# Queries over the ALiBi slope, and one VectorE operation that adds the distance, multiplies by the slope and gathers the rows' greatest attention scores

## The chip, the core and the metric

The kernel runs on one core of a Trainium2 chip. Its engines work side by side and wait for each other by semaphores: TensorE (PE in the profile; its weight loads are PEld), VectorE (DVE), ScalarE (ACT), GpSimd (POOL) and SyncE (SP, which issues most DMAs). The metric is device time in microseconds for one execution of the whole program.

## What is computed

One step of a hybrid decoder layer for a prompt of 512 rows and 64 sample rows (8 sequences of 8): a modulated RMSNorm, one input projection, a gated short convolution beside a sliding-window attention, a merge by gates, an output projection, then a convolutional feed-forward block. The change concerns the attention alone: 16 query heads in 4 groups of 4, a window of 128 keys, a penalty that grows with the distance (ALiBi, one slope per head) and one learned sink per head:

```
s = jnp.einsum('...qhgd,...khd->...hgqk', q, k).astype(jnp.float32) * (HEAD_DIM ** -0.5)
s = s - _alibi_slopes()[:, :, None, None] * dist[..., None, None, :, :]
s = jnp.where(valid[..., None, None, :, :], s, NEG_INF)
m = jnp.maximum(jnp.max(s, axis=-1, keepdims=True), sink)
p = jnp.exp(s - m)
p = p / (jnp.sum(p, axis=-1, keepdims=True) + jnp.exp(sink - m))
```

## The kernel before

Activations lie transposed (features on the 128 partitions, 576 columns of tokens). Each product with a weight matrix runs as three products of high and low parts, so every weight tile is first split: ScalarE rounds the high part (`whi`), VectorE or a DMA that adds makes the low part (`wlo`). TensorE runs nearly without a pause, in the order in which the program is written (`pinned` keeps it so); the order on VectorE, ScalarE and GpSimd is set by a scheduler that simulates the program while it is built.

The attention runs as a filler between the matmuls of the input projection. `tick` is called after each group of six matmuls and lets the generator `attention` take a step at a fixed rate. The prompt part has 16 turns: 4 key heads times 4 blocks of 128 queries (block 0 has 128 keys, the others 256). In each turn `prompt_scores` multiplies 4 query heads by the keys into two PSUM tiles (`aux`) and makes 4 score tiles `s` by one VectorE operation per head, which multiplies the distance table `nd` (minus the distance, or a very large negative number where a key is not allowed) by the slope and adds the scores. `softmax_exps` reduces them to the rows' greatest values, negated (`nmx`), takes the minimum with the negated sinks, runs four exponentials on ScalarE that also sum up the rows (`den`), and one for the sink (`es`); `divide` multiplies the scores by 1/`den`. A turn later `prompt_turn` transposes `s` on TensorE, and a turn after that `prompt_values` multiplies by the values. After the prompt, two decode passes for the sample rows do the same with tables of their own (`nds`, slopes `slo` and sinks `snks` per partition).

`queries` makes the attention's queries from the projection: it scales the product into a high part on ScalarE, the low part on VectorE, and an unsplit copy for the sample rows on VectorE (`qS`, `qX`). A DMA on GpSimd's queue puts the low part beside the high one.

Lines that the text speaks of: the score operations are lines 1096 (prompt) and 1025 (decode), the reductions 954, the minimum 957, the exponentials 960, the sink's exponential 966 with its input `es` on line 965, the sum 969, the reciprocal 970, the division 972. The transposes and all operations that go through a recording helper have line 115; value products have line 1122. ScalarE's first tap of the convolution is `y<-pad`, VectorE's taps are operations that read and write `y`.

Of the kernel before, what the change touches and what calls it, by code (L numbers as in the profile page):

```python
# [10 lines left out]
F32 = mybir.dt.float32  # L11
F32R = mybir.dt.float32r
AF = mybir.ActivationFunctionType
# [62 lines left out]
def step_kernel(ctx: ExitStack, tc: tile.TileContext, ins: dict, outs: list):  # L76
# [19 lines left out]
    def slot(s, dt=F32, shape=None):  # L96
        return ap_.tile(shape or [P, NT], dt, tag="a", name=nm(s))
# [4 lines left out]
    def aux():  # L102
        return pa.tile([P, 512], F32, tag="aux", name=nm("aux"))
# [27 lines left out]
    def pv(t):  # L131
        return t[:, 0:512]
# [671 lines left out]
    def key_parts(hd):  # L804
# [5 lines left out]
            nc.gpsimd.dma_start(x[other].bitcast(F32), x[mine].bitcast(F32))  # L810
        KS[hd] = kh, kl

    def queries(t, ps=None):

        scale = HD**-0.5 if ps is None else 1.0
        if ps is None:
            ps = product(weights(kpm(w_in, Q0 + t * P), NK), h)
        low = slot("low", F32R, [P, 512])
        hd, g2 = t // 2, t % 2
        qq = [slot("q", F32R, [P, 512]) for _ in range(2)]  # L820
        for par in range(2):
            nc.scalar.activation(qq[par][HALF[par]], pv(ps)[HALF[par]], AF.Copy, scale=scale)
        for par in range(2):
            q, mine, other = qq[par], HALF[par], HALF[1 - par]
            nc.vector.scalar_tensor_tensor(
                out=low[mine], in0=pv(ps)[mine], scalar=scale, in1=q[mine].bitcast(F32),
                op0=ALU.mult, op1=ALU.subtract,
            )
            nc.gpsimd.dma_start(q[other].bitcast(F32), low[mine].bitcast(F32))
            QS[4 * hd + 2 * g2 + par] = q  # L830
            ready[hd] = ticks[0] + Q_TICKS
            dst = qS[:, hd // 2, :, :, par, g2, :] if par == hd % 2 else qX[:, hd // 2, :, :, g2, :]
            nc.vector.tensor_scalar(
                out=dst[mine], in0=sv(ps)[mine].rearrange("p (q b t) -> p q b t", q=2, b=4),
                scalar1=scale, scalar2=None, op0=ALU.mult,
            )
# [69 lines left out]
    nds = con2[:, 0:512].rearrange("p (q c) -> p q c", q=2)  # L906
    ind = con2[:, 512:516]
    slo = con2[:, 516:520]
    nsnk = cp.tile([P, 16], F32, tag="nsnk", name="nsnk")
    nc.vector.tensor_scalar(out=nsnk, in0=snk, scalar1=-1.0, scalar2=None, op0=ALU.mult)  # L910
    snks = cp.tile([P, 4], F32, tag="snks", name="snks")
    sel = cp.tile([P, 4, 4], F32, tag="sel", name="sel")
    nc.vector.tensor_tensor(
# [3 lines left out]
        op=ALU.mult,  # L917
    )
    nc.vector.reduce_sum(out=snks, in_=sel, axis=AX.X)
    nsnks = cp.tile([P, 4], F32, tag="nsnks", name="nsnks")  # L920
    nc.vector.tensor_scalar(out=nsnks, in0=snks, scalar1=-1.0, scalar2=None, op0=ALU.mult)
    par2 = cp.tile([74, P], F32, tag="par2", name="par2")
    for dst, src in (
        (par2[:66], ins["ffn_conv_w"].rearrange("o a (r c) -> (o a r) c", c=P)),
# [18 lines left out]
    pinned.append(pe)  # L943
    ot = [wp.tile([P, 4, NT], F32, tag="oh", name=nm("o"), bufs=2) for _ in range(2)]

    def softmax(s, n, sinks, nsinks, w):
        softmax_exps(s, n, sinks, nsinks, w)()

    def softmax_exps(s, n, sinks, nsinks, w):


        nmx = sp.tile([P, n], F32, tag="nmx", name=nm("nmx"))
        for x in range(n // 2):
            nc.vector.tensor_reduce(
                out=nmx[:, 2 * x : 2 * x + 2], in_=s[x][:, :, :w], axis=AX.X, op=ALU.max, negate=True
            )
        nc.vector.tensor_tensor(out=nmx, in0=nmx, in1=nsinks, op=ALU.min)
        den = sp.tile([P, n], F32, tag="den", name=nm("den"))
        for x in range(n):
            nc.scalar.activation(  # L960
                s[x // 2][:, x % 2, :w], s[x // 2][:, x % 2, :w], AF.Exp,
                bias=nmx[:, x : x + 1], accum_out=den[:, x : x + 1],
            )
# [12 lines left out]

        return divide
# [13 lines left out]
    def decode_scores(q, s, cV):  # L991
        kTc = []
        for raw, v in (caches[q][:2], caches[q][2:]):
            cV.append(v)
            a = aux()
            for b in range(2):
                for j in range(2):
                    at = (b * 2 + j) * P
                    transpose(a[:, at : at + P], raw[:, b, j * P : j * P + P], ident)
            t = slot("kTc", shape=[P, 2, 2, P])  # L1000
            nc.scalar.copy(t.rearrange("p b j w -> p (b j w)"), a)
            kTc.append(t)
            yield False
        s += [slot("s", shape=[P, 2, 256]) for _ in range(2)]
        S = [aux() for _ in range(2)]
        for j in range(2):
            at = j * 256
            lhs = qS[:, j, q].rearrange("p b x g t -> p (b x g t)")
            for b in range(4):
                for hf in range(2):  # L1010
                    matmul(
                        S[hf][32 * b : 32 * b + 32, at : at + P],
                        lhs[HALF[hf], 32 * b : 32 * b + 32],
                        kTc[b // 2][HALF[hf], b % 2, j, :],
                        start=True, stop=True,
                    )
            for hf in range(2):
                matmul(
                    S[hf][:, at + P : at + 2 * P], lhs[HALF[hf]], tok_cols(kT[j][HALF[hf]], 4),
                    start=True, stop=True,  # L1020
                )
        for j in range(2):
            for hf in range(2):
                hd, at = 2 * j + hf, j * 256
                nc.vector.scalar_tensor_tensor(
                    out=s[j][:, hf, :], in0=nds[:, q, :], scalar=slo[:, hd : hd + 1],
                    in1=S[hf][:, at : at + 256], op0=ALU.mult, op1=ALU.add,
                )
        yield False
        divide = softmax_exps(s, 4, snks, nsnks, 256)  # L1030
        yield False
        yield False
        divide()
        yield False
# [48 lines left out]
    def prompt_scores(hd, i, ss):  # L1083
        w = 256 if i else P
        k0 = (i - 1) * P if i else 0
        ss += [slot("s", shape=[P, 2, 256]) for _ in range(2)]
        kh, kl = (x[:, k0 : k0 + 256] for x in KS[hd])
        for x in range(2):
            S = aux()
            for e in range(2):  # L1090
                q = QS[4 * hd + 2 * x + e][:, i * P : i * P + P]
                dst = S[:, e * 256 : e * 256 + 256]
                matmul(dst, q, kh, start=True, stop=False)
                matmul(dst, q, kl, start=False, stop=True)
            for e in range(2):
                nc.vector.scalar_tensor_tensor(
                    out=ss[x][:, e, :w], in0=nd[:, 256 - w : 256],
                    scalar=2.0 ** (-8.0 * (4 * hd + 2 * x + e + 1) / 16),
                    in1=S[:, e * 256 : e * 256 + w], op0=ALU.mult, op1=ALU.add,
                )  # L1100

    def prompt_turn(hd, i, ss):
# [32 lines left out]
    def attention():  # L1135
# [3 lines left out]
        for n in range(19):  # L1139
            arg = (n // 4, n % 4) if n < 16 else None  # L1140
            if n in CACHE_AT:
                cache_load(CACHE_AT.index(n))
            if arg:
                yield from prompt_ready(*arg)
            ready_values = turned
            turned = (*waiting[:2], prompt_turn(*waiting)) if waiting else None
            waiting, scored = scored, (*arg, []) if arg else None
            if arg:
                prompt_scores(*scored)
            yield False  # L1150
            if ready_values:
                prompt_values(*ready_values)
            if arg:
                h4 = slice(4 * arg[0], 4 * arg[0] + 4)
                softmax(scored[2], 4, snk[:, h4], nsnk[:, h4], 256 if arg[1] else P)
            yield False
        filler[1] = CX_RATE
        waiting = None
# [1025 lines left out]
```

## Time and profile before

| | |
|---|---|
| median of 3 runs | 975.87 us (975.84 to 975.96) |
| the profiled execution | 975.77 us |
| its span, first to last instruction | 974.0 us |
| TensorE matmul busy | 960.2 us (99%) |
| VectorE busy | 699.9 us (72%) |
| ScalarE busy | 529.8 us (54%) |
| GpSimd busy | 156.9 us (16%) |
| TensorE's granted clock, mean of the span | 0.997 |

The page also follows the chain of work that ended last back from the last instruction; 95% of it is TensorE. A busy share is an average over the span, so the timelines are needed to see who waits where. Starts in a timeline are us from the span's start; neighbouring instructions of one engine overlap a little, so that four in a row take less than four times one.

### The profile page before, as it was taken

What the parts mean: (1) busy time and instruction counts of PE and PEld (TensorE: products, weight loads), DVE (VectorE), ACT (ScalarE), POOL (GpSimd) and SP (SyncE); (2) the same over time, 40 slices, a digit from 0 to 9 for tenths busy, and PEclk for the clock granted to TensorE, in tenths of its full rate; (3) what the DMA queues carried; (4) which work ended last, traced back from release to release, by engine and by line L of the source; (5) the groups of instructions that cost most, each with busy time, mean ns of one, the idle gap of its engine ahead of it and who ended that gap; (6) DMA issues with size and microseconds to landing.
All of it is one profiled execution on the core that took longest, in us unless ns stands there. A gap on an engine that the chain in (4) does not pass through costs nothing.

```text
span 974.0 us, 18976 instructions
## 1 busy us (share of the span) xinstructions
PE 960.2 (99%) x7396; PEld 924.6 (95%) x7396; DVE 699.9 (72%) x1359; ACT 529.8 (54%) x968; POOL 156.9 (16%) x349
## 2 busy tenths in 40 slices
PE   7999999999999999999999999999999999999997
PEld 5899999999999889999899999999999999999996
DVE  5555877777968658897588687784568873578753
ACT  6365667656654435665343568662347652256553
POOL 2132222111212000011000131220013220022120
PEclk9999999999999999999999999999999999999998
DMA  9994345464466772478953454672447762556502
GB/s 302 318 265 123 97 96 124 107 192 106 124 151 182 228 236 86 112 154 223 355 195 90 123 126 98 159 179 87 117 124 169 165 162 66 133 135 166 131 9 98
DMA packets 183563, 148.82 MB, mean 153 GB/s; under 512 B 8007, under 2 KB 161966, under 8 KB 183186
## 3 DMA queue, kind: packets, MB, share of 16 engines
q1 hardware_dynamic: 169954, 108.83, 36.6%
q0 software_dynamic: 13088, 38.00, 19.3%
q8 instruction: 58, 0.95, 0.4%
q10 hardware_dynamic: 432, 0.79, 0.2%
q14 instruction: 31, 0.25, 0.1%
HBM read 109.17 MB, written 7.35 MB: 120 GB/s over the span
## 4 chain that ended last, share of the span: by engine, by line
PE 95%; DMA 2%; issue 1%; SPq 1%; DVE 0%; POOL 0%; ACT 0%; POOLq 0%; DVEq 0%
PE mm L115 64%; PE aux L115 28%; PE aux L1223 2%; PE aux L1122 1%; DMA ad<-in_w_ada 1%; SPq L437 1%; DMA x<-in_x_prompt 1%; POOL r L115 0%; ACT hh L115 0%; DVE hl L115 0%; DVE yo L115 0%; POOLq L2180 0%; DVEq L2180 0%; DVE xn L115 0%; DVE modT L115 0%
## 5 line engine op out<-in xcount | busy, mean ns | idle before, releaser
L115 ACT ACTIVATE whi<-raw 128x1024 fp32r<-128x1024 f32 (+2 forms) x176 | 179.8, 1031 | 94.5 <-PE mm L115 46.7
L115 DVE TENSOR_TENSOR wlo<-raw,whi 128x1024 fp32r<-128x1024 f32 (+2 forms) x133 | 157.0, 1183 | 52.3 <-ACT whi L115 50.7
L115 POOL DMA_DIRECT2D wlo<-raw x43 | 37.7, 876 | 374.4 <-ACT wlo L115 203.7
L115 PE MATMUL mm<-hh,whi 128*128 128x256 f32 (+2 forms) x392 | 92.4, 302 | 0.6 <-ACT hh L115 0.6
L115 PE MATMUL mm<-hh,wlo 128*128 128x256 f32 (+2 forms) x392 | 89.4, 294 | 0.0
L115 PE MATMUL mm<-hl,whi 128*128 128x256 f32 (+2 forms) x392 | 88.1, 295 | 0.3 <-DVE hl L115 0.2
L115 PE MATMUL mm<-th,whi 128*128 128x288 f32 x296 | 87.8, 297 | 0.0
L115 PE MATMUL mm<-tl,whi 128*128 128x288 f32 x296 | 87.2, 295 | 0.0
L115 PE MATMUL mm<-th,wlo 128*128 128x288 f32 x296 | 87.2, 295 | 0.0
L115 PEld LDWEIGHTS mm<-hh,whi 128*128 128x128 f32 x392 | 65.8, 188 | 9.1 <-issue 7.5
L115 PEld LDWEIGHTS mm<-hh,wlo 128*128 128x128 f32 x392 | 67.2, 188 | 0.3 <-DVE wlo L115 0.3
L115 PEld LDWEIGHTS mm<-hl,whi 128*128 128x128 f32 x392 | 66.1, 188 | 1.0 <-DVE hl L115 1.0
L115 PE MATMUL mm<-fh,whi 128*128 128x256 f32 (+1 forms) x304 | 65.4, 296 | 0.0
L115 PE MATMUL mm<-fl,whi 128*128 128x256 f32 (+1 forms) x304 | 65.3, 296 | 0.0
L115 PE MATMUL mm<-fh,wlo 128*128 128x256 f32 (+1 forms) x304 | 64.8, 294 | 0.0
L115 DVE SCALAR_TENSOR_TENSOR x<-mm,modT,x 128x512 f32<-128x512 f32 (+1 forms) x29 | 19.6, 677 | 62.2 <-PE mm L115 62.0
L115 PEld LDWEIGHTS mm<-th,whi 128*128 128x128 f32 x296 | 55.6, 188 | 0.8 <-issue 0.8
L115 PEld LDWEIGHTS mm<-tl,whi 128*128 128x128 f32 x296 | 55.7, 188 | 0.0
L115 PEld LDWEIGHTS mm<-th,wlo 128*128 128x128 f32 x296 | 55.7, 188 | 0.0
L115 DVE TENSOR_TENSOR raw<-raw 128x512 f32<-128x512 f32 x74 | 51.2, 692 | 2.5
L115 PEld LDWEIGHTS mm<-fh,wlo 128*128 128x128 f32 x304 | 51.0, 188 | 0.0
L115 PEld LDWEIGHTS mm<-fl,whi 128*128 128x128 f32 x304 | 50.9, 189 | 0.0
(369 smaller groups left out, 2915.7 us busy)
## 6 DMA issues: line engine op xcount, KB each, us to landing
raw<-in_w_in SPq DMA_DIRECT2D x52, 512.0 KB, 4.7
raw<-in_w_up SPq DMA_DIRECT2D x44, 512.0 KB, 4.3
wlo<-raw POOLq DMA_DIRECT2D x43, 512.0 KB, 4.7
ada<-in_w_ada SPq DMA_DIRECT2D x64, 256.0 KB, 5.6
ad<-in_w_ada SPq DMA_DIRECT2D x32, 256.0 KB, 5.9
raw<-in_w_down SPq DMA_DIRECT2D x16, 512.0 KB, 4.1
wl<-s POOLq DMA_DIRECT2D x27, 256.0 KB, 4.3
raw<-in_w_conv_out SPq DMA_DIRECT2D x8, 512.0 KB, 4.5
```

Of the source, the lines that this page charges most:

```text
L115: done = getattr(self.engine, name)(*args, **kwargs)
L437: return tc.keep_in_program_order(queue.dma_start(dst, src))
L1122: done = nc.tensor.matmul(O[HALF[par], :256], vt(i - nkt + 1 + kt)[:, hd * 64 : hd * 64 + 64], pts[kt][:, par * 256 : par * 256 + 256], st ...
L1223: done = nc.tensor.matmul(ps[32 * j : 32 * j + 32, :], cT[:, k, :], cols[k][j], start=(k == 1), stop=(k == NK - 2),)
```

## The change

The queries are divided by the head's slope where they are scaled, so that TensorE gives scores over the slope. A new helper `biased` replaces the scale-and-add operation: it adds the distance table, multiplies by the slope, and gathers in the same pass the greatest value of each row, starting from the sink, into a column of `mx`. `softmax_exps` takes `mx` times -1 instead of the reductions and the minimum. The negated copies of the sinks (`nsnk`, `nsnks`) go.

```diff
+    def slope(head):
+        return 2.0 ** (-8.0 * (head + 1) / 16)
...
-            nc.scalar.activation(qq[par][HALF[par]], pv(ps)[HALF[par]], AF.Copy, scale=scale)
+            nc.scalar.activation(
+                qq[par][HALF[par]], pv(ps)[HALF[par]], AF.Copy, scale=scale / slope(2 * t + par)
+            )
...
-                out=low[mine], in0=pv(ps)[mine], scalar=scale, in1=q[mine].bitcast(F32),
+                out=low[mine], in0=pv(ps)[mine], scalar=scale / slope(2 * t + par),
+                in1=q[mine].bitcast(F32),
...
-                scalar1=scale, scalar2=None, op0=ALU.mult,
+                scalar1=scale / slope(2 * t + par), scalar2=None, op0=ALU.mult,
...
-    nc.vector.tensor_scalar(out=nsnk, in0=snk, scalar1=-1.0, scalar2=None, op0=ALU.mult)
...
-    nc.vector.tensor_scalar(out=nsnks, in0=snks, scalar1=-1.0, scalar2=None, op0=ALU.mult)
...
+    def biased(out, dist, scores, slopes, sink, greatest):
+        nc.vector.tensor_tensor_reduce(
+            out=out, in0=dist, in1=scores, scale=slopes, scalar=sink, op0=ALU.add, op1=ALU.max,
+            accum_out=greatest,
+        )
...
-        for x in range(n // 2):
-            nc.vector.tensor_reduce(
-                out=nmx[:, 2 * x : 2 * x + 2], in_=s[x][:, :, :w], axis=AX.X, op=ALU.max, negate=True
-            )
-        nc.vector.tensor_tensor(out=nmx, in0=nmx, in1=nsinks, op=ALU.min)
+        nc.vector.tensor_scalar(out=nmx, in0=mx, scalar1=-1.0, scalar2=None, op0=ALU.mult)
...
-                nc.vector.scalar_tensor_tensor(
-                    out=s[j][:, hf, :], in0=nds[:, q, :], scalar=slo[:, hd : hd + 1],
-                    in1=S[hf][:, at : at + 256], op0=ALU.mult, op1=ALU.add,
+                biased(
+                    s[j][:, hf, :], nds[:, q, :], S[hf][:, at : at + 256], slo[:, hd : hd + 1],
+                    snks[:, hd : hd + 1], mx[:, hd : hd + 1],
                 )
...
-                nc.vector.scalar_tensor_tensor(
-                    out=ss[x][:, e, :w], in0=nd[:, 256 - w : 256],
-                    scalar=2.0 ** (-8.0 * (4 * hd + 2 * x + e + 1) / 16),
-                    in1=S[:, e * 256 : e * 256 + w], op0=ALU.mult, op1=ALU.add,
+                y = 2 * x + e
+                biased(
+                    ss[x][:, e, :w], nd[:, 256 - w : 256], S[:, e * 256 : e * 256 + w],
+                    slope(4 * hd + y), snk[:, 4 * hd + y : 4 * hd + y + 1], ss[2][:, y : y + 1],
                 )
```

TensorE's instructions and SyncE's are the same, in the same order, in both programs. On the other engines the scheduler orders some anew. Three places, all in block 2 of head 0, are shown; the numbers behind names are buffers, and differ between the programs.

VectorE, from the last score operation of block 2 to the next convolution tap, before:

```order
L1096 SCALAR_TENSOR_TENSOR s_1267<-con_927,aux_1275 128x256 x2
L954 TENSOR_REDUCE nmx_1300<-s_1266 128x2
L954 TENSOR_REDUCE nmx_1300<-s_1267 128x2
L1340 TENSOR_TENSOR pad_1318<-mm_1210,c_1018 128x512
L1341 TENSOR_TENSOR pad_1318<-mm_1210,c_1018 128x8x8
L115 TENSOR_TENSOR wlo_1704<-raw_1701,whi_1703 128x1024
L957 TENSOR_TENSOR nmx_1300<-nmx_1300,nsnk 128x4
L115 SCALAR_TENSOR_TENSOR y_1325<-pad_1318,parT,y_1325 128x592
```

and after (`ISA` is the new operation; it is followed each time by a second instruction that writes one column of `mx`):

```order
L952 ISA s_1261,mx_1262<-con_927,aux_1270,snk 128x256
L952 ISA mx_1262 128x1
L964 TENSOR_SCALAR nmx_1295<-mx_1262 128x4
L1350 TENSOR_TENSOR pad_1311<-mm_1206,c_1014 128x512
L1351 TENSOR_TENSOR pad_1311<-mm_1206,c_1014 128x8x8
L972 TENSOR_TENSOR es_1302<-snk,nmx_1295 128x4
L115 TENSOR_TENSOR wlo_1694<-raw_1691,whi_1693 128x1024
L115 SCALAR_TENSOR_TENSOR y_1318<-pad_1311,parT,y_1318 128x592
```

The greatest value `nmx` stood behind a weight split and now stands ahead of it, straight behind the last of four such pairs.

ScalarE at the same place, from a weight's high part to the copies of the transposed block before, before:

```order
L115 ACTIVATE whi_1703<-raw_1701 128x1024
L115 ACTIVATE y_1325<-pad_1318,parT 128x592
L115 ACTIVATE kh_1329<-kT_727 64x512
L960 ACTIVATE s_1266,den_1304<-s_1266,nmx_1300 128x256 x2
L960 ACTIVATE s_1267,den_1304<-s_1267,nmx_1300 128x256 x2
L1113 COPY pt_1371<-aux_1366 128x512
L966 ACTIVATE es_1309<-es_1309 128x4
```

and after:

```order
L115 ACTIVATE whi_1693<-raw_1691 128x1024
L967 ACTIVATE s_1260,den_1297<-s_1260,nmx_1295 128x256 x2
L967 ACTIVATE s_1261,den_1297<-s_1261,nmx_1295 128x256 x2
L115 ACTIVATE y_1318<-pad_1311,parT 128x592
L115 ACTIVATE kh_1322<-kT_727 64x512
L973 ACTIVATE es_1302<-es_1302 128x4
L1122 COPY pt_1364<-aux_1359 128x512
```

The four exponentials moved ahead of the convolution's first tap (`y`) and the key split (`kh`).

VectorE from block 3's last scores to block 2's division, before:

```order
L1096 SCALAR_TENSOR_TENSOR s_1381<-con_927,aux_1389 128x256 x2
L969 TENSOR_TENSOR den_1304<-den_1304,es_1309 128x4
L954 TENSOR_REDUCE nmx_1418<-s_1380 128x2
L954 TENSOR_REDUCE nmx_1418<-s_1381 128x2
L970 RECIPROCAL den_1304<-den_1304 128x4
L957 TENSOR_TENSOR nmx_1418<-nmx_1418,nsnk 128x4
L972 TENSOR_SCALAR s_1266<-s_1266,den_1304 128x256 x2
L972 TENSOR_SCALAR s_1267<-s_1267,den_1304 128x256 x2
```

and after, the start of this stretch and its end:

```order
L115 TENSOR_TENSOR kl_1323<-kT_727,kh_1322 64x512
L976 TENSOR_TENSOR den_1297<-den_1297,es_1302 128x4
L952 ISA s_1373,mx_1375<-con_927,aux_1376,snk 128x256
L952 ISA mx_1375 128x1
```

```order
L952 ISA s_1374,mx_1375<-con_927,aux_1383,snk 128x256
L952 ISA mx_1375 128x1
L977 RECIPROCAL den_1297<-den_1297 128x4
L964 TENSOR_SCALAR nmx_1412<-mx_1375 128x4
L979 TENSOR_SCALAR s_1260<-s_1260,den_1297 128x256 x2
L979 TENSOR_SCALAR s_1261<-s_1261,den_1297 128x256 x2
```

The sum `den`, which waits for ScalarE, moved ahead of block 3's score operations, and the second convolution tap stands between their pairs; the reductions are gone.

## Rows read from the trace of the kernel before

**Rows 1.** The page, part 1: busy us (share of the span) x instructions, each engine.

```profile
PE 960.2 (99%) x7396; PEld 924.6 (95%) x7396; DVE 699.9 (72%) x1359; ACT 529.8 (54%) x968; POOL 156.9 (16%) x349
```

**Rows 2.** TensorE's waits, 21 to 974 us: us in total, times, longest.

```profile
PE mm L115 <- ACT hh L115: 0.6, 2, 0.5
PE mm L115 <- DVE hl L115: 0.2, 1, 0.2
PE mm L115 <- ACT sq L115: 0.2, 1, 0.2
```

**Rows 3.** Busy time in the attention's stretch: window, us, engines, PEclk, DMA share, GB/s.

```profile
80.00:262.00 182.00, 182.00 (x1445) 169.93 (x1444) 141.91 (x379) 115.94 (x293) 34.12 (x72) 1.00 0.47 120
```

**Rows 4.** VectorE's groups by form: busy us, mean ns of one | idle before.

```profile
L954 DVE TENSOR_REDUCE nmx<-s 128x2 f32<-128x512 f32 x28 | 18.0, 676 | 0.0
L1096 DVE SCALAR_TENSOR_TENSOR s<-con,aux 128x256 f32<-128x256 f32 x48 | 17.2, 415 | 6.7 <-PE aux L115 6.5
...
L1096 DVE SCALAR_TENSOR_TENSOR s<-con,aux 128x128 f32<-128x128 f32 x16 | 3.8, 284 | 4.9 <-PE aux L115 4.9
...
L954 DVE TENSOR_REDUCE nmx<-s 128x2 f32<-128x256 f32 x8 | 2.9, 408 | 0.0
...
L957 DVE TENSOR_TENSOR nmx<-nmx,nsnk 128x4 f32<-128x4 f32 x16 | 2.5, 159 | 0.2
```

**Rows 5.** VectorE's timeline around blocks 2 and 3 of head 0: start us, us.

```profile
99.26 1.42 DVE L1096 SCALAR_TENSOR_TENSOR s<-con,aux 128x256 f32<-128x256 f32 x4
...
102.51 1.22 DVE L115 TENSOR_TENSOR wlo<-raw,whi 128x1024 fp32r<-128x1024 f32 x1
...
105.89 1.40 DVE L1096 SCALAR_TENSOR_TENSOR s<-con,aux 128x256 f32<-128x256 f32 x4
...
108.67 1.14 DVE L972 TENSOR_SCALAR s<-s,den 128x256 f32<-128x256 f32 x4
```

**Rows 6.** The same view: VectorE's smallest memset, ScalarE's accumulator read, its smallest operation.

```profile
L441 DVE MEMSET first<- 128x1 f32 x1 | 0.1, 59 | 0.8 <-PEq L2169 0.8
...
L960 ACT ACTIVATION_READ_ACCUMULATOR s<-s,nmx 128x1 f32 x72 | 13.5, 188 | 0.0
...
L966 ACT ACTIVATE es<-es 128x4 f32<-128x4 f32 x18 | 3.5, 192 | 0.0
```

**Rows 7.** Timelines: transposes of blocks 2, 3 and head 1's block 0; block 3's division.

```profile
111.69 1.03 PE L115 MATMUL aux<-ident,s 128*128 128x128 f32 x8
...
120.27 1.04 PE L115 MATMUL aux<-ident,s 128*128 128x128 f32 x8
...
128.98 0.60 PE L115 MATMUL aux<-ident,s 128*128 128x128 f32 x4
...
116.71 1.13 DVE L972 TENSOR_SCALAR s<-s,den 128x256 f32<-128x256 f32 x4
```

**Rows 8.** ScalarE's timeline, block 2: first tap, first and last exponential.

```profile
102.69 0.79 ACT L115 ACTIVATE y<-pad,parT 128x592 f32<-128x592 f32 x1 [1.30 <-DVE pad L1341]
...
103.91 0.49 ACT L960 ACTIVATE s<-s,nmx 128x256 f32<-128x256 f32 x1
...
105.39 0.50 ACT L960 ACTIVATE s<-s,nmx 128x256 f32<-128x256 f32 x1
```

**Rows 9.** VectorE's groups by form: two SBUF sources, scalar-tensor-tensor and plain.

```profile
L115 DVE SCALAR_TENSOR_TENSOR y<-pad,par2T,y 128x592 f32<-128x592 f32 x44 | 36.6, 833 | 6.8 <-ACT y L115 5.4
...
L115 DVE TENSOR_TENSOR ol<-o,oh 128x576 fp32r<-128x576 f32 x8 | 5.8, 754 | 0.9 <-ACT oh L115 0.9
```

**Rows 10.** The page, part 3, the queue that brings instructions: packets, MB, share.

```profile
q8 instruction: 58, 0.95, 0.4%
```

**Rows 11.** Waits of TensorE's weight loads, 78 to 265 us; one timeline row with its releaser.

```profile
PEld mm L115 <- issue: 5.4, 14, 0.4
...
PEld aux L1122 <- issue: 2.3, 14, 0.2
...
141.46 0.20 PEld L1122 LDWEIGHTS aux<-pt,V 128*64 128x64 f32 x4 [0.16 <-DVE den L970]
```

More of the change, by code (lines that the diff above doesn't have):

```diff
@@ L908, in step_kernel @@
     slo = con2[:, 516:520]
-    nsnk = cp.tile([P, 16], F32, tag="nsnk", name="nsnk")
-    nc.vector.tensor_scalar(out=nsnk, in0=snk, scalar1=-1.0, scalar2=None, op0=ALU.mult)
     snks = cp.tile([P, 4], F32, tag="snks", name="snks")
@@ L919, in step_kernel @@
     nc.vector.reduce_sum(out=snks, in_=sel, axis=AX.X)
-    nsnks = cp.tile([P, 4], F32, tag="nsnks", name="nsnks")
-    nc.vector.tensor_scalar(out=nsnks, in0=snks, scalar1=-1.0, scalar2=None, op0=ALU.mult)
     par2 = cp.tile([74, P], F32, tag="par2", name="par2")
@@ L944, in step_kernel, with softmax, softmax_exps @@
     ot = [wp.tile([P, 4, NT], F32, tag="oh", name=nm("o"), bufs=2) for _ in range(2)]
-    def softmax(s, n, sinks, nsinks, w):
-        softmax_exps(s, n, sinks, nsinks, w)()
-    def softmax_exps(s, n, sinks, nsinks, w):
-        nmx = sp.tile([P, n], F32, tag="nmx", name=nm("nmx"))
-        for x in range(n // 2):
-            nc.vector.tensor_reduce(
-                out=nmx[:, 2 * x : 2 * x + 2], in_=s[x][:, :, :w], axis=AX.X, op=ALU.max, negate=True
-            )
-        nc.vector.tensor_tensor(out=nmx, in0=nmx, in1=nsinks, op=ALU.min)
+    def biased(out, dist, scores, slopes, sink, greatest):
[3 more added lines that the diff above has]
+        )
+    def softmax(s, mx, n, sinks, w):
+        softmax_exps(s, mx, n, sinks, w)()
+    def softmax_exps(s, mx, n, sinks, w):
+        nmx = sp.tile([P, n], F32, tag="nmx", name=nm("nmx"))
+        nc.vector.tensor_scalar(out=nmx, in0=mx, scalar1=-1.0, scalar2=None, op0=ALU.mult)
         den = sp.tile([P, n], F32, tag="den", name=nm("den"))
@@ L1004, in decode_scores @@
         s += [slot("s", shape=[P, 2, 256]) for _ in range(2)]
+        mx = sp.tile([P, 4], F32, tag="mx", name=nm("mx"))
         S = [aux() for _ in range(2)]
@@ L1024, in decode_scores @@
                 hd, at = 2 * j + hf, j * 256
-                nc.vector.scalar_tensor_tensor(
-                    out=s[j][:, hf, :], in0=nds[:, q, :], scalar=slo[:, hd : hd + 1],
-                    in1=S[hf][:, at : at + 256], op0=ALU.mult, op1=ALU.add,
+                biased(
+                    s[j][:, hf, :], nds[:, q, :], S[hf][:, at : at + 256], slo[:, hd : hd + 1],
+                    snks[:, hd : hd + 1], mx[:, hd : hd + 1],
                 )
         yield False
-        divide = softmax_exps(s, 4, snks, nsnks, 256)
+        divide = softmax_exps(s, mx, 4, snks, 256)
         yield False
@@ L1086, in prompt_scores @@
         ss += [slot("s", shape=[P, 2, 256]) for _ in range(2)]
+        ss.append(sp.tile([P, 4], F32, tag="mx", name=nm("mx")))
         kh, kl = (x[:, k0 : k0 + 256] for x in KS[hd])
@@ L1154, in attention @@
                 h4 = slice(4 * arg[0], 4 * arg[0] + 4)
-                softmax(scored[2], 4, snk[:, h4], nsnk[:, h4], 256 if arg[1] else P)
+                *s, mx = scored[2]
+                softmax(s, mx, 4, snk[:, h4], 256 if arg[1] else P)
             yield False
```

## The prediction

> **What bounds the kernel now.** I read the page's busy times first, then TensorE's waits, then the stretch of the attention, then the instructions that the change touches, and last the timelines around the point where attention hands its result back to TensorE. TensorE's matmuls fill 960.2 us of a span of 974.0 us [rows 1]. From 21 us to the end TensorE waits for another engine 1.0 us in all, in five places, and none of these is an attention tile [rows 2]. The change acts between about 80 and 262 us. [...] So VectorE work here costs time only if its result comes too late for TensorE, and saving it gains only where TensorE now waits for it, which is nowhere. I also read TensorE's own instruction list: apart from line numbers it is the same before and after, matmul for matmul.
>
> **What goes.** VectorE loses 36 greatest-score reductions: 28 of 128x512 at 676 ns and 8 of 128x256 at 408 ns, 18.0 + 2.9 = 20.9 us [rows 4]. The 18 small minimum operations of 159 ns become 18 small multiplications by -1 of the same 128x4 size, taken at the same price, so nothing. Two negations of the sinks go once per program, 0.3 us at that price. VectorE loses 21.2 us in all.
>
> **What comes.** The 72 scale-and-add operations (64 in the prompt, 8 in the decode rows) turn into 72 operations that add, scale and keep the greatest value, each followed by a second instruction that only writes a 128x1 result. The trace has neither of the two.
> - *The main operation* reads the same two tiles and writes the same one, so the nearest rows are the ones it replaces: 415 ns at 128x256, 284 ns at 128x128 [rows 4]. Four of them take 1.42 us [rows 5], so one follows another after (1.42 - 0.415) / 3 = 0.335 us. From below I take no gain, since the elements are the same. From above I let it run at half the rate: 415 - 284 = 131 ns for 128 elements, so 0.26 us more at 256.
> - *The 128x1 write* lies between 59 ns (a 128x1 memset, which reads no tile) and 188 ns (ScalarE's read of its accumulator, which does the same job there) [rows 6]. That ScalarE read costs what a tiny ScalarE operation costs, 192 ns; by analogy I take VectorE's tiny operation, 0.16 us [rows 4, 6]. That is 72 x 0.16 = 11.5 us, with ends at 4.2 and 13.5 us.
>
> VectorE: 699.9 - 21.2 + 11.5 = **690 us busy** (683 to 692; at half rate up to about 19 us more).
>
> The factor in the queries costs nothing: the same 16 ScalarE and 32 VectorE instructions get another constant. The scores come out of TensorE divided by the slope in the same number of matmuls.
>
> **What lies on TensorE's path.** Per block of 128 queries the chain is: scores from TensorE, four score operations, the greatest value, four exponentials on ScalarE, the row sum, the division on VectorE, then TensorE's transpose of the result. The closest hand-over is block 2 of head 0. Its division ends at 108.67 + 1.14 = 109.81 us and the transpose starts at 111.69 us, a margin of 1.88 us [rows 5, 7]. The next closest that I found is block 3, 116.71 + 1.13 = 117.84 against 120.27 us: 2.43 us [rows 7].
>
> Block 2 after the change, worked through in the new order:
> - Its four pairs start no later than now, 99.26 us [rows 5], and need 4 x (0.335 + 0.16) = 1.98 us. With the multiplication by -1 the greatest value is there at 101.4 us. Now it comes only after two reductions and a weight split that ends at 102.51 + 1.22 = 103.7 us; in the new order that split stands behind it.
> - ScalarE now runs the exponentials ahead of the convolution's first tap and the key split. By the present rows the exponentials take 105.39 + 0.50 - 103.91 = 1.98 us, tap and split 103.91 - 102.69 = 1.22 us [rows 8]. So exponentials end at 103.4, tap and split at 104.6, the sink's small exponential at 104.8.
> - The row sum waits for that one. It now stands ahead of block 3's scores in VectorE's queue; that is the wait that the change adds. Behind it are the block 3 pairs, a tap and the division, and behind those TensorE's transpose. The sum is done at 105.1 at the earliest, and I put it at 105.6, behind VectorE's tap and key split; block 3's first operation starts at 105.89 us today [rows 5], so it loses nothing.
> - From 105.8 us: four pairs 1.98, a tap 0.83 [rows 9], reciprocal and negation 0.3, division 1.14. It ends at 110.0 us, 0.2 us later than now and **1.7 us before the transpose**.
>
> Thus VectorE is emptier, but the latency at this place hardly changes: the second tap and the pairs stand where the reductions stood. With the read at 59 ns the division ends about 0.8 us earlier (eight reads), with 188 ns 0.2 us later. TensorE waits for none of these.
>
> VectorE also feeds TensorE the low weight halves. The one in this stretch starts at 102.51 us and is first used just ahead of the transposes at 128.98 us [rows 5, 7], so 0.6 us either way is nothing. SP's queue keeps its order; on POOL's, one weight addition moves ahead of its neighbours.
>
> **Sum:** 975.77 us (the profiled execution: span 974.0 and 1.8 around it) - 0 + 0 = **975.8 us**. The median of the runs shown is 975.87, 0.1 above that execution. A measurement of this kernel can tell about 0.2% (2.0 us) from no change.
>
> **Rivals.**
> 1. *The new pair is slow, and the division comes late for TensorE: slower.* At block 2 the extra time counts eight times, four pairs ahead of the exponentials and four ahead of the division. It decides from 1.7 / 8 = 0.21 us per pair on. At half rate (0.26 us more) the division ends at 110.0 + 2.1 = 112.1 us and TensorE waits 0.4 us there and, with 2.43 us at the next place, nothing: 976.2 us, still no change to a measurement. With a pair of 1.0 us (0.5 more) it is 4.0 - 1.7 = 2.3 us at block 2, and perhaps as much again over the later blocks: 978 to 980 us. For it: no row shows the instruction. Against it: the element count is the same, and a scalar-tensor-tensor operation of 592 elements with both sources in SBUF takes 833 ns against 754 ns for a plain one of 576, so nothing like half rate [rows 9]. [...] Chance 0.05.
> 2. *The engine has to be given the new operation's program in each execution: slower by a constant.* The instruction list shows an operation that the program before does not contain. The nearest row is the queue that brings instructions: 0.95 MB in 0.4% of sixteen engines' span, 0.004 x 974 = 3.9 us [rows 10]. Between 0 and 3.9 us would be added, up to 979.7 us. Against it: TensorE's first wait is for the input, and a load could hide there. Chance 0.03. [...]
> 3. *TensorE has hidden waits that a quicker softmax removes: faster.* Its weight loads pause 14 times for 0.16 us ahead of the value products and 14 times for 0.39 us behind them, and one such pause is put down to VectorE [rows 11]. If all were waits, 14 x 0.55 = 7.7 us would go: 968.1 us. Against it: the pauses are equally long whoever is named, most have no releaser, and 2.3 + 5.4 us of them are put to issue. Chance 0.02.
> 4. *The change saves VectorE nothing,* because a read costs as much as its share of the reductions, 20.9 / 72 = 0.29 us. The time is the same 975.8 us. It lies inside the forecast.
>
> **How the numbers follow.** The forecast, no TensorE wait added or removed, with rival 4 and the half-rate case inside it, has 0.90, rivals 1 to 3 the other 0.10. Of the 0.08 of rivals 1 and 2, 0.07 is slower by over 0.2% and 0.01 too small to tell. Faster by over 0.2% gets 0.03: the 0.02 of rival 3 and 0.01, taken from the forecast, for something unseen. Within 0.2% is left with 0.90. The range runs from 975.3 (half of the 1.0 us of waits gone) to 977.0 (the half-rate wait of 0.4 us, and as much again at two more blocks); that leaves out less than 2 in 10.
>
> **What would show it.** Right: line 952 shows 72 operations of about 415 and 284 ns with 72 writes of about 160 ns; VectorE near 690 us busy; TensorE busy all of 80 to 262 us; no wait of TensorE on an attention tile; the transposes of block 2 still near 111.7 us, its division ending near 110. Wrong: a transpose that waits for VectorE (rival 1), a longer span ahead of the first matmul or more time around the span (rival 2), value products without their pauses (rival 3).

## The result and the profile after

The changed kernel took 977.60 us (median of 14 runs, 977.19 to 978.09) against 975.86 us (14 runs, 975.27 to 976.26): a ratio of 1.0019, 95% interval 1.0011 to 1.0026. It is 1.74 us slower, every run of it above every run of before. The forecast was 975.8 us with a range to 977.0, so the result lies 0.6 us outside. The profiled execution took 978.07 us, 2.30 us more than that of before and 0.5 us above its own median.

The page after, part 1, against [rows 1]:

```profile
PE 962.2 (99%) x7396; PEld 925.9 (95%) x7396; DVE 686.5 (70%) x1393; ACT 530.1 (54%) x968; POOL 155.9 (16%) x349
```

VectorE lost 13.4 us, TensorE's matmuls became 2.0 us longer in the sum, in the same number. TensorE's waits from 21 to 974 us (us in total, times, longest), against [rows 2]:

```profile
PE mm L115 <- ACT hh L115: 0.8, 1, 0.8
PE mm L115 <- ACT sq L115: 0.2, 1, 0.2
```

That is 1.0 us as before, and no attention tile. The attention's stretch, against [rows 3]:

```profile
80.00:262.00 182.00, 182.00 (x1444) 169.92 (x1444) 129.31 (x416) 116.74 (x295) 34.02 (x72) 1.00 0.47 119
```

TensorE is busy all of it at the same clock; VectorE has 12.6 us more to spare. VectorE's groups after, by form, against [rows 4]:

```profile
L952 DVE CUSTOM_DVE_ANT_0 s<-con,aux,snk 128x256 f32<-128x256 f32 x48 | 20.2, 475 | 3.9 <-PE aux L115 3.7
...
L952 DVE DVE_READ_ACCUMULATOR2_ANT mx<- 128x1 f32 x72 | 5.9, 82 | 0.0
L952 DVE CUSTOM_DVE_ANT_0 s<-con,aux,snk 128x128 f32<-128x128 f32 x16 | 4.6, 344 | 5.7 <-PE aux L115 5.6
L952 DVE CUSTOM_DVE_ANT_0 s<-con,aux,snks 128x256 f32<-128x256 f32 x8 | 3.9, 540 | 1.0 <-PE aux L115 1.0
```

The fused operation costs 60 ns more than the one it replaces at either size of the prompt, and its read 82 ns. The timeline of block 2 of head 0, VectorE and then TensorE, against [rows 5, 7]:

```profile
99.86 0.48 DVE L952 CUSTOM_DVE_ANT_0 s<-con,aux,snk 128x256 f32<-128x256 f32 x1
100.27 0.08 DVE L952 DVE_READ_ACCUMULATOR2_ANT mx<- 128x1 f32 x1
100.27 0.48 DVE L952 CUSTOM_DVE_ANT_0 s<-con,aux,snk 128x256 f32<-128x256 f32 x1
...
109.15 1.15 DVE L979 TENSOR_SCALAR s<-s,den 128x256 f32<-128x256 f32 x4
...
112.78 1.03 PE L115 MATMUL aux<-ident,s 128*128 128x128 f32 x8
```

The read hides behind the next operation: from one start to the next it is 0.41 us. The division ends at 110.30 us, 2.48 us ahead of the transposes. But the transposes, the hand-over that the prediction watched, start at 112.78 us and not 111.69. So TensorE was 1.09 us late on arrival, with no wait in between that names the attention.

**Where the time came from.** Three groups of TensorE serve as marks in all runs: these transposes (M1), the last transposes of the decode rows (M2, behind the last changed instruction), and the row sums near the end (M3). M2 and M3 in TensorE's timeline before:

```profile
262.37 1.03 PE L115 MATMUL aux<-ident,s 128*128 128x128 f32 x8
...
965.30 0.51 PE L115 MATMUL mm<-ones,acc 128*128 128x2 f32 x4
```

and after:

```profile
263.46 1.04 PE L115 MATMUL aux<-ident,s 128*128 128x128 f32 x8
...
967.72 0.51 PE L115 MATMUL mm<-ones,acc 128*128 128x2 f32 x4
```

From M1 to M2 both take 150.68 us: the stretch that the change edits costs nothing. The 2.42 us at M3 are 1.09 us from ahead of the attention and 1.33 us from M2 to M3 (702.93 us before, 704.26 after), where no instruction and no order of instructions differs.

The early part is in the transfers. Those between 10 and 27 us of the span, before:

```profile
DMA packets 6690, 5.93 MB, mean 349 GB/s; under 512 B 311, under 2 KB 6662, under 8 KB 6688
```

and after:

```profile
DMA packets 6221, 5.59 MB, mean 329 GB/s; under 512 B 299, under 2 KB 6196, under 8 KB 6219
```

In the same 17 us 0.34 MB less arrives, and TensorE, which starts on these transfers, starts its projection 1.15 us later. Its first matmul of the projection, before and after:

```profile
27.30 0.53 PE L115 MATMUL mm<-hh,whi 128*128 128x256 f32 x2
```

```profile
28.45 0.53 PE L115 MATMUL mm<-hh,whi 128*128 128x256 f32 x2
```

### The profile page after: what moved, and what is told of

It is laid out like the page before. It is cut to its first block, busy times and chain, and to the rows that moved or that the text cites. A ratio compares the mean times of both kernels' runs of the same rounds, so it can differ in the third digit from the quotient of the medians.

```text
span 976.3 us, 19014 instructions
## 1 busy us (share of the span) xinstructions
PE 962.2 (99%) x7396; PEld 925.9 (95%) x7396; DVE 686.5 (70%) x1393; ACT 530.1 (54%) x968; POOL 155.9 (16%) x349
## 4 chain that ended last, share of the span: by engine, by line
PE 95%; DMA 2%; issue 1%; DVE 0%; SPq 0%; POOL 0%; ACT 0%; POOLq 0%; DVEq 0%
PE mm L115 64%; PE aux L115 28%; PE aux L1233 2%; PE aux L1131 1%; DMA ad<-in_w_ada 1%; DMA raw<-in_w_in 1%; DMA x<-in_x_prompt 1%; SPq L437 0%; POOL r L115 0%; ACT hh L115 0%; DVE hl L115 0%; DVE yo L115 0%; POOLq L2190 0%; DVEq L2190 0%; DVE xn L115 0%
```

## The experiments

Theory A: the new operation's presence in the program costs the time (the prediction's rival 2). B: the program's length or layout. C: chance of loading. D: the 72 uses. E came out of the first four runs, F out of e5 to e8. Each difference below is the median against that of the kernel before, run on the same chip in the same batch.

**e1, the kernel before loaded again.**

> The kernel before, nothing edited, loaded as a program of its own beside the kernel before. It measures what the same program gives when it is loaded again. The changed kernel is 1.74 us above the kernel before (977.60 against 975.86 us), 1.1 us of it before the first changed instruction runs. Theory A, the new operation's presence in the program costs the time: 0 here, within 0.3 us. Theory B, a program that is longer or laid out otherwise reaches its data later: 0 here. Theory C, each load of a program falls on other addresses by chance and so lands its first transfers earlier or later: a difference of either sign here, up to 1 or 2 us.

975.88 against 975.74 us, ratio 1.0000 (0.9992 to 1.0009); M1 111.72, M3 965.34. C falls.

**e2, one fused operation, no more.**

```diff
-    nc.vector.tensor_scalar(out=nsnks, in0=snks, scalar1=-1.0, scalar2=None, op0=ALU.mult)
+    big = cp.tile([P, 1], F32, tag="big", name="big")
+    nc.vector.tensor_tensor_reduce(
+        out=nsnks, in0=snks, in1=snks, scale=-0.5, scalar=snks[:, 0:1], op0=ALU.add, op1=ALU.max,
+        accum_out=big,
+    )
```

> The kernel before with one instruction exchanged: the negated sinks of the decode heads (128x4) are formed by the fused operation instead of a multiplication. No other instruction moves on any engine. Theory A, the operation's presence is what costs: about +1.1 us, all of it ahead of 27 us of the span, or +1.7 us if the slow drift later in the span also hangs on its presence. Theory B (length or layout of the program): 0 within 0.3 us, as the program is no longer than before by more than one instruction. Theory D (72 uses of it in the attention cost the time): 0.

976.60 us, +0.86 (ratio 1.0009, 1.0000 to 1.0017), M1 at 112.37: near the 1.1 us that A foretold.

**e3, the changed kernel without the fused operation.**

```diff
-        nc.vector.tensor_tensor_reduce(
-            out=out, in0=dist, in1=scores, scale=slopes, scalar=sink, op0=ALU.add, op1=ALU.max,
-            accum_out=greatest,
-        )
+        nc.vector.scalar_tensor_tensor(
+            out=out, in0=dist, scalar=slopes, in1=scores, op0=ALU.mult, op1=ALU.add,
+        )
+        nc.vector.tensor_reduce(out=greatest, in_=out, axis=AX.X, op=ALU.max)
...
-        nc.vector.tensor_scalar(out=nmx, in0=mx, scalar1=-1.0, scalar2=None, op0=ALU.mult)
+        nc.vector.tensor_tensor(out=nmx, in0=mx, in1=sinks, op=ALU.max)
+        nc.vector.tensor_scalar(out=nmx, in0=nmx, scalar1=-1.0, scalar2=None, op0=ALU.mult)
```

It leaves out the multiplication of the scores by the slope.

> The changed kernel with each fused operation taken apart into ordinary ones: the multiply-add of before (distance times slope plus score) and a maximum over that one head, and the sinks taken into the maximum by an operation of their own. Left out: the scores are not multiplied by the slope any more, so the numbers are others, the amount of work is not less. VectorE gets 72 more reductions of one head each (about 0.25 to 0.4 us each), where the margin ahead of TensorE was 1.7 us at the tightest block, so up to 1 us of waits in the attention may appear. Theory A: no offset ahead of 27 us, total 0 to +1 us by the waits alone. Theory B: the offset of about 1.1 us ahead of 27 us stays, since the program is longer than before by about as many instructions as the changed one or more. Theory D: 0 ahead of 27 us.

976.74 us, +1.00 (1.0009, 1.0000 to 1.0018), M1 at 112.50, so the early loss is there without the operation. This speaks against A and for B.

**e4, 72 tiny writes,** one ahead of each score operation, in the prompt as in the decode rows (one place shown).

```diff
+                nc.vector.memset(mx[:, e : e + 1], 0.0)
                 nc.vector.scalar_tensor_tensor(
```

> The kernel before with 72 tiny writes (a 128x1 memset ahead of each score operation) added on VectorE, some 59 ns each by the row of before, 4 us of VectorE time in all with no one waiting for them. Theory A: 0 within 0.3 us. Theory B: +1 us or so ahead of 27 us of the span, as in the changed kernel, since the program is as much longer. Theory C: either sign.

975.74 us, +0.00, M1 at 111.34. B falls too. What sets e2, e3 and the changed kernel apart from before, e1 and e4 is memory: before, e1 and e4 have the same resident tiles ahead of the weight buffers; e2 adds one, e3 and the changed kernel drop `nsnk` and `nsnks`. In the built program `nsnks` (16 bytes) and e2's `big` (4 bytes) take 32 bytes each, so e2 adds 32 and the change takes away 64 + 32. The weight buffers began at byte 151,040 of each partition (590 times 256), and begin at 150,944 after the change. These four buffers for raw weights lie 4,096 bytes apart, so they all leave the multiples of 256 together; the 57 buffers of the common pool lie 2,400 bytes apart and begin at eight different places past such a multiple in either program.

**e5 to e9, e15, e16: theory E, the address.** One edit, the tile of the decode heads' sinks made longer by columns that no one reads, in the changed kernel (32 and 96 bytes) and in the one before (32, 64, 128, 256 and 512 bytes); no instruction moves:

```diff
-    snks = cp.tile([P, 4], F32, tag="snks", name="snks")
+    snks = cp.tile([P, 12], F32, tag="snks", name="snks")[:, 0:4]
```

> The changed kernel with the tile of the decode heads' sinks 32 bytes longer (8 more columns that nobody reads). No instruction differs; all buffers behind this tile in SBUF lie 32 bytes further on, which puts them back on multiples of 64 bytes. Theory E (the two removed tiles, nsnk and nsnks, took 96 bytes with them and left the buffers of the transfers at 32 past a multiple of 64, where each transfer takes longer): the offset ahead of 27 us falls from about 1.1 us to within 0.4 us of none, the share of queue q1 from 37.5% to 36.7%, and the time by 0.8 to 1.7 us, to 975.9 to 976.8 us. Theory A (the operation's presence): no change, 977.6 us.

> The kernel before with the same tile 32 bytes longer: nothing else, no new operation, no instruction moved; the buffers behind it lie at 32 past a multiple of 64. Theory E: +0.7 to +1.1 us (as the kernel with one instruction exchanged, whose extra tile also took 32 bytes), share of q1 up from 36.6% to 37.6%. Theory A: 0.

> The kernel before with that tile 64 bytes longer: the buffers move but stay on multiples of 64 bytes (no longer of 128 and above). Theory E with 64 bytes as the unit: 0 within 0.3 us, share of q1 36.7%. If any move of the buffers cost the time, or if multiples of 128 counted: +0.7 us or more.

> The changed kernel with that tile 96 bytes longer, which gives every buffer behind it the address it had in the kernel before. Theory E: the same time as with 32 bytes (975.9 to 976.8 us). What is left above 975.8 us, if anything, belongs to the fused operation and its use in the attention (theory D) and not to the addresses; the drift of 1.2 us between 266 and 944 us of the profiled run is the place to look.

> The kernel before with the tile of the decode heads' sinks 512 bytes longer, so that the weight buffers, which began at a multiple of 512 bytes (295 times 512), begin at one again (296 times 512). So far a shift of 32 bytes cost 0.84 us and one of 64 bytes 0.48 us. Theory E (a transfer's packets, of 512 bytes for the weight columns, take longer where they do not start on such a multiple): 0 within 0.3 us, packets of 512 bytes ahead of 45 us at 27 ns as before, share of q1 36.6%. If any shift of the buffers costs: +0.5 to +0.9 us.

> The kernel before with the sinks' tile 256 bytes longer, which puts the weight buffers in the middle between two multiples of 512 bytes. Theory E with 512 bytes as the unit: +0.4 to +0.9 us, share of q1 37.5%, packets of 512 bytes ahead of 45 us at 31 to 32 ns. Theory E with 256 bytes as the unit: 0 within 0.3 us, 36.6%, 27 ns.

> The kernel before with the sinks' tile 128 bytes longer. Unit of 128 bytes: 0 within 0.3 us, share of q1 36.6%. Unit of 256 or 512 bytes: +0.4 to +0.9 us, 37.5%.

| kernel | weight buffers, bytes past a multiple of 256 | M1 | M2 | M3 | M2 to M3 | median against before | ratio, interval |
|---|---|---|---|---|---|---|---|
| before | 0 | 111.69 | 262.37 | 965.30 | 702.93 | | |
| e15, before + 256 | 0 | 111.72 | 262.40 | 965.33 | 702.93 | -0.05 | 0.9998, 0.9989 to 1.0007 |
| e9, before + 512 | 0 | 111.66 | 262.34 | 965.24 | 702.90 | -0.15 | 0.9997, 0.9988 to 1.0006 |
| e6, before + 32 | 32 | 112.48 | 263.17 | 966.19 | 703.02 | +0.84 | 1.0009, 1.0000 to 1.0018 |
| e7, before + 64 | 64 | 112.14 | 262.80 | 965.81 | 703.01 | +0.48 | 1.0005, 0.9996 to 1.0014 |
| e16, before + 128 | 128 | 112.67 | 263.31 | 966.33 | 703.02 | +1.02 | 1.0010, 1.0001 to 1.0019 |
| changed | 160 | 112.78 | 263.46 | 967.72 | 704.26 | +1.74 | 1.0019, 1.0011 to 1.0026 |
| e5, changed + 32 | 192 | 112.79 | 263.51 | 967.78 | 704.27 | +1.85 | 1.0020, 1.0011 to 1.0029 |
| e8, changed + 96 | 0 | 111.69 | 262.40 | 966.62 | 704.22 | +1.33 | 1.0014, 1.0005 to 1.0023 |

Multiples of 64 were the wrong unit (e5 and e7 missed), and so were multiples of 512 (e15); 256 bytes is the one that fits all nine. e8 missed its time as well, 977.17 us where at most 976.8 was expected: what is left there is the subject of theory F. The median alone does not tell e7 from the kernel before (its interval includes 1.0000); the marks do. In the kernels on multiples of 256, the runs below included, M1 lies between 111.34 and 111.81 us (without e17, where TensorE waits); in the seven off them between 112.14 and 112.79.

The transfers of 10 to 27 us with the buffers moved by 128 bytes (e16):

```profile
DMA packets 6459, 5.73 MB, mean 337 GB/s; under 512 B 299, under 2 KB 6445, under 8 KB 6457
```

and by 256 (e15):

```profile
DMA packets 6914, 6.01 MB, mean 354 GB/s; under 512 B 309, under 2 KB 6896, under 8 KB 6912
```

Over all runs it is 5.93 to 6.10 MB on multiples of 256 and 5.59 to 5.80 MB off them. The kernel before, moved by 128 bytes, loses bandwidth as the changed one does; moved by 256 it does not. So A and D explain nothing of the early part: e2 paid 0.86 us for the 32 bytes of its extra tile, as e6 paid 0.84 us for 32 bytes without any new operation. Address restored, the changed kernel reaches M1 at 111.69 us, M2 0.03 us late, and then drifts as the changed kernel does, 1.29 us against 1.33 (e8).

**e10 to e14, e18: theory F, the deal of the buffers.** Behind M2 only one thing differs in the programs of before and e8: which buffer each tile got. Some 360 of about 1,450 tiles lie elsewhere, 60 of them in the raw weight buffers and the rest in the pool of 57. (86 tiles of a few columns lie elsewhere too; they do so in e4, which takes 702.94 us from M2 to M3.) The numbers behind names in the lists of instructions count tiles and don't show the deal. The scheduler, which prices the attention otherwise, frees the tiles there in another order, and the deal stays shuffled to the end. A tile taken for one tiny write deals anew:

```diff
                 prompt_values(*ready_values)
+            if n % 4 == 2:
+                z = slot("z")
+                nc.gpsimd.memset(z[:, 0:1], 0.0)
             if arg:
```

with `n % 4 == 2` in e10 and e11 (five tiles, where the expectations say four), `n == 8` in e13 and e14, `n % 4 == 3` in e18; in e12 the tile is one of the four raw weight buffers, taken behind the prompt heads.

> The kernel before with four dummy tiles taken from the pool of 57 buffers during the attention (one tiny write on GpSimd each); no other instruction moves on any engine, but from there on 358 of some 1,400 tiles lie in other buffers of the pool than before. Theory F (the drift of 1.2 to 1.3 us behind the attention, where no instruction differs, comes from which buffer each tile got): no offset ahead of 80 us, and a drift of either sign, 0.3 to 1.5 us, behind 260 us. Theory D (the drift belongs to the fused operation): 0 within 0.3 us throughout.

> The changed kernel with the addresses of before (the tile 96 bytes longer; 977.17 us when it ran) and with the same four dummy tiles, which deal the pool's buffers anew. Theory F: the drift behind 260 us is another one than 1.3 us, by 0.3 us or more to either side. Theory D: 977.2 us again within 0.3 us, drift 1.2 to 1.3 us.

> The changed kernel with the addresses of before and one dummy tile from the four raw weight buffers behind the prompt heads' attention; 56 weight tiles from there on lie in another of the four buffers, nothing else moves. Theory F with the raw buffers as the cause: the drift changes by 0.3 us or more. Theory F with the pool of 57 alone, and theory D: 977.2 us again within 0.3 us.

> The changed kernel with the addresses of before and one dummy tile from the pool of 57, taken at the ninth turn of the attention: 169 tiles change their buffers, no instruction moves. Theory F (the buffers dealt decide the drift behind the attention): a third value of the drift, anywhere from 0 to 1.5 us, so 975.8 to 977.4 us, and not both 977.2 us in total and the same course over the span as without the dummy. Theory D (the fused operation makes the drift, and the four dummies of the earlier run took it away by chance of another kind): 977.2 us with the same course.

> The kernel before with the same one dummy tile: 158 tiles change their buffers. Theory F: a drift behind the attention of up to 1 us, of either sign, without the fused operation in the program; the four dummies gave a bulge of 0.35 us between 450 and 800 us of the span that was given back. Theory D: the offset stays within 0.1 us of none throughout.

> The changed kernel with the addresses of before and four dummy tiles taken at other turns of the attention, a fourth deal of its buffers (382 tiles move, no instruction). The deals so far gave 977.17, 976.84 and 976.04 us. Theory F: a value of its own between 975.7 and 977.3 us, its difference from the others made behind 260 us of the span alone. Theory D: 977.2 us.

**e17, 72 uses with the deal of before** (24 tiles elsewhere); the place in the prompt, and the decode rows have the same:

```diff
+                nc.vector.tensor_tensor_reduce(
+                    out=mx[:, e : e + 1], in0=snk[:, e : e + 1], in1=snk[:, e : e + 1],
+                    scale=1.0, scalar=snk[:, e : e + 1],
+                    op0=ALU.add, op1=ALU.max, accum_out=gr[:, e : e + 1],
+                )
                 nc.vector.scalar_tensor_tensor(
```

> The kernel before with the fused operation put in 72 times on one column (128x1, its result read by no one), one ahead of each score operation; all work of before is still done, and only 24 of some 1,400 tiles lie in other buffers than before. VectorE gets 72 more operations with their reads, some 0.15 to 0.3 us a pair by the rows of the changed kernel, so 10 to 20 us of VectorE time with 1.7 us of margin at the tightest block: waits of up to 1 us inside the attention (80 to 260 us of the span) may appear. Theory D (72 uses of the operation make the drift): +1.0 us or more behind 260 us. Theory F: within 0.3 us of no drift behind 260 us.

| kernel | fused operations | M1 | M2 | M3 | M2 to M3, against 702.93 | median against before | ratio, interval |
|---|---|---|---|---|---|---|---|
| e8, changed, its own deal | 72 | 111.69 | 262.40 | 966.62 | +1.29 | +1.33 | 1.0014, 1.0005 to 1.0023 |
| e12, raw buffers redealt | 72 | 111.44 | 262.15 | 966.40 | +1.32 | +1.35 | 1.0013, 1.0004 to 1.0022 |
| e13, second deal | 72 | 111.53 | 262.17 | 966.21 | +1.11 | +1.09 | 1.0011, 1.0002 to 1.0020 |
| e11, third deal | 72 | 111.75 | 262.48 | 965.83 | +0.42 | +0.28 | 1.0003, 0.9994 to 1.0012 |
| e18, fourth deal | 72 | 111.45 | 262.18 | 965.26 | +0.15 | -0.13 | 0.9999, 0.9990 to 1.0008 |
| e10, before redealt | 0 | 111.77 | 262.38 | 965.37 | +0.06 | -0.06 | 0.9999, 0.9990 to 1.0008 |
| e14, before, another deal | 0 | 111.81 | 262.47 | 965.80 | +0.40 | +0.40 | 1.0003, 0.9994 to 1.0012 |
| e3, without the operation | 0 | 112.50 | 263.18 | 966.61 | +0.50 | +1.00 | 1.0009, 1.0000 to 1.0018 |
| e17, deal of before | 72 | 114.87 | 265.58 | 968.63 | +0.12 | +3.19 | 1.0035, 1.0021 to 1.0049 |

With the operation kept and the buffers dealt anew the drift goes from 1.29 to 0.15 us; with 72 uses and nearly the old deal it is 0.12 us. D falls, F stands. Another deal of the four raw buffers changed nothing (e12).

The marks come from one execution each, but behind M1 these repeat closely: e1 keeps its offset of 0.03 us to M3, e15 and e9 take 702.93 and 702.90 us from M2 to M3, and the changed kernel, e5, e8 and e12, which share the deal of the pool, 704.22 to 704.27. The intervals of e10, e11, e14 and e18 include 1.0000, so their medians alone would not tell them from the kernel before; e8 and e18 lie apart by them too. F missed once: for e10 it foretold 0.3 us or more, and 0.06 is left at M3. That is a net figure. Compared matmul by matmul with the kernel before, e10 falls back by 0.36 us from M2 to 600 us of the span and makes it up again; e18 falls back by 0.67 us to 550 us, nearly as far as e8 (0.78), and gains 0.5 us behind.

e17 is slower inside the attention, by a division that comes late, as in the prediction's rival 1. TensorE's waits in 80 to 262 us there:

```profile
PE aux L115 <- DVE s L972: 2.1, 3, 1.7
```

and VectorE's groups of the added pair:

```profile
L1105 DVE CUSTOM_DVE_ANT_0 mx<-snk 128x1 f32<-128x1 f32 x64 | 10.5, 216 | 0.0
...
L1105 DVE DVE_READ_ACCUMULATOR2_ANT old<- 128x1 f32 x64 | 5.4, 84 | 0.0
```

In the timeline a pair takes less than the 216 + 84 ns, since the read overlaps the next operation:

```profile
98.88 0.24 DVE L1105 CUSTOM_DVE_ANT_0 mx<-snk 128x1 f32<-128x1 f32 x1
99.02 0.10 DVE L1105 DVE_READ_ACCUMULATOR2_ANT old<- 128x1 f32 x1
99.02 0.22 DVE L1105 CUSTOM_DVE_ANT_0 mx<-snk 128x1 f32<-128x1 f32 x1
...
105.82 1.14 DVE L972 TENSOR_SCALAR s<-s,den 128x256 f32<-128x256 f32 x4
```

From start to start that is 0.14 us, below the 0.21 us from which rival 1 was to decide. The pairs do harm because they are bunched: they read nothing that the attention makes, and the scheduler let all 72 start between 79.6 and 104.2 us, 20 of them behind 98.8 us. Block 1's division starts at 105.82 us there (97.95 before), late for its transposes, and M1 moves by 3.18 us. So e17 shows what a late division costs, and not that the new pair is slow enough to make one. In the changed kernel the fused operation adds 60 ns and takes the reductions away, and nothing is late.

## Why the prediction was wrong, point by point

- **What bounds the kernel, and that the attention's VectorE work lies beside it:** right. TensorE is busy for 182.00 us of the stretch before and after, M1 to M2 takes the same 150.68 us, and e18, with all of the change's instructions, the old addresses and another deal, runs at 0.9999 of before.
- **VectorE's sum:** right; 686.5 us against 690 (683 to 692). The main operation was taken at no extra and costs 60 ns more, inside its bounds of 0 and 131 (260 at 128x256), so the half rate assumed for the upper bound is shown by no run; the read was taken at 160 ns, behind the operation, and costs 82 ns, hidden. From start to start a pair takes 0.41 us where 0.495 was summed, so the division left 2.48 us where 1.7 was forecast.
- **Rival 1** did not come about; e17 shows that a late division does hold TensorE up (2.1 us of waits). **Rival 2**, a constant for the new operation's program, is what the result looked like, and e2 alone would have seemed to prove it; e6 shows the same 0.84 us from 32 bytes and no new operation. Its sign, a longer span ahead of the first matmul, is absent: that matmul starts at 4.85 us before and 4.81 after. **Rival 3:** the pauses of TensorE's weight loads behind the value products are the same 5.4 us in 14 as in [rows 11]. **Rival 4** no: VectorE saved 13.4 us.
- **The failed step** is the sum, "- 0 + 0". It counts instructions and their order. "Two negations of the sinks go once per program, 0.3 us at that price" priced two instructions and left out the two tiles that they wrote. These took 96 bytes, and without them the weight buffers began 160 bytes past a multiple of 256: +1.09 us ahead of M1 in the profiled execution. The second omission is in the same step: "TensorE's own instruction list ... is the same before and after" was read as if equal lists took equal time, but the tiles behind the names had been dealt other buffers: +1.33 us behind M2. Together 2.42 us in the profiled execution, which is one of the slower of its kernel; the medians differ by 1.74. By medians the address has the smaller share: put right (e8) it leaves 1.33 of 1.74 us, or of the 1.85 us of e5 in the same batch, so 0.4 to 0.5 us, and the deal of e18 takes away the rest.
- **The range** had no term for either. Its top, 977.0, came from late hand-overs alone.

The packets themselves took longer. Those of 512 bytes ahead of 45 us took 27.1 ns in the mean before, 31.2 ns moved by 32 bytes, 32.1 by 128, 32.2 in the changed kernel and 32.5 at 192. The unit is read from the marks: moves by 256 and 512 bytes left M1 at 111.72 and 111.66 us, starts 32 to 192 bytes past a multiple of 256 put it at 112.14 to 112.79. What happens in a transfer off such a multiple is not shown.

What stays open is how the deal acts. In the median the transfers behind M2 are issued no later in e8 than the matmuls themselves have slipped; in the changed kernel, which shares its deal of the pool, SyncE's 196 issues there come 1.73 us later in the median and the matmuls beside them 1.74. The extra time is spread over the 5,330 matmuls from M2 to M3: from one start to the next none differs by more than 15 ns from the kernel before, some are longer and some shorter, and the mean is 0.24 ns more. In e8 the 3,283 whose own operands had not moved became 0.29 ns longer in the mean, the 1,686 whose moving operand alone had moved 0.11 ns; in e14 it is the other way round, 0.01 ns for 4,151 that had not moved and 0.29 ns for 1,000 whose moving operand had. So a matmul's own operand does not explain it, and which access disturbs it wasn't tried. Nor was the changed kernel tried with exactly the old deal, since the scheduler sets it.

No version is faster than the kernel before: e9 (975.61 us against 975.76) and e18 (975.76 against 975.89) are furthest below it, and neither differs from it beyond its interval.

## What to carry to other kernels

Price the storage of an edit as well as its instructions: a small resident tile that comes or goes moves every buffer behind it, here by 96 bytes. Where short weight rows are loaded on the path, see whether the time falls with their buffers at a multiple of 256 bytes: the rows of 512 bytes here took 27.1 ns a packet at one and 31.2 to 32.5 ns 32 to 192 bytes past one. Before a difference of 0.1 or 0.2% is put down to an edit, move the old kernel's buffers by as much, or deal them anew, and see whether it moves too. Marks at the same matmuls in both traces (ahead of the changed stretch, behind it, at the end) tell in one look whether the changed stretch has anything to do with it.

## What was not expected of the hardware

- Thirty-two bytes in the start of a buffer cost nearly as much as 128: packets of 512 bytes went from 27.1 to 31.2 ns, and the kernel's median rose by 0.84 us (1.02 with 128 bytes, 0.48 with 64). In the profiled execution 0.79 us of it lie ahead of M1, though the shift concerns every weight load of the program (behind M1 it is hidden: M1 to M3 grows by 0.10 us in e6).
- The pace of TensorE's matmuls behind M2, 702.93 us of them, differed by 1.14 us (0.16%) between e8 and e18, whose programs differ there by the buffers of the pool alone, at the same granted clock (0.998 in the mean of either span). Between M2 and M3 no wait of TensorE is in the profile of the kernel before, nor in that of the changed one, which shares e8's deal of the pool.
- VectorE's fused operation took 216 ns for one column (e17), 344 for 128 and 475 for 256, by estimate from the three some 0.2 us and 1 ns a column. With the slope read from a tile, as in the decode rows, it took 540 ns at 256 columns. Its accumulator read, 82 ns, starts together with the next operation (both at 100.27 us in block 2).
